# Retention as steps of one pipeline, with ACT and DVE in written order and each head's norm ahead of its output projection

## The chip, the cores and the metric

One core of a Trainium2 chip runs the whole kernel in one launch. The metric is the device time of that core in microseconds (us), the median over runs. Its engines work side by side, each through its own queue in order: TensorE (PE; its weight loads are shown as PEld), VectorE (DVE), ScalarE (ACT), GpSimd (POOL), and SyncE (SP), which here only issues DMAs. DMAs can be issued from the queues of SP, ACT and POOL. They meet at semaphores.

## The reference

A block of a transformer: a feed-forward part, a mixer, a second feed-forward part and a last norm, for 512 tokens behind 16 meta tokens (T = 528), width 1024, in fp32. The change lies in the mixer, in its retention:

```python
rq = rope(rq.reshape(B, T, RET_HEADS, RET_DK), pos)                       # 4 heads of 256
rk = rope(rk.reshape(B, T, RET_HEADS, RET_DK), pos) * (RET_DK ** -0.5)
yr = retention(rq, rk, rv)              # per head: (q k^T * decay) v, then per token
                                        # y = y * rsqrt(mean(y * y) + EPS) over the head's 512 columns
yr = (jax.nn.silu(rg) * yr) @ w_ret_out
...
ya = dsa_attention(aq, ak, av, iq, ik, iw, k_top) @ w_att_out
merged = jax.nn.sigmoid(g_ret) * yr + jax.nn.sigmoid(g_att) * ya
return merged @ w_mix_out
```

(axes' transpositions left out.) The attention picks for each query 128 keys by an index score of 8 small heads, `sum_h iw_h * relu(iq_h . ik)`; the score and the selection are computed beside the retention, ahead of the attention.

## The kernel before

All products are fp32 in three passes: each operand is split into a high part of the matmul's type and the rest (`split`: ACT copies the high part, DVE subtracts it, L117 and L118), and `mm3` (L145) adds high x high, high x low and low x high into PSUM. So each 128 columns of weights (`raw`, loaded by `load_w` on SP's queue, two buffers) go through one ACT and one DVE instruction to `whi` and `wlo` (three buffers each) ahead of their 24 matmuls.

The stages follow one another: feed-forward 1, the dense projections (values of retention and attention, index queries, queries and keys of head 0), the retention with index scores and selection beside it, the attention with its 8 heads, the output projections, feed-forward 2. In feed-forward and the dense projections the order of PE, ACT and DVE is written out (`manual_schedule(engines=BUSY)`): `steps_through` (L283) walks a list of steps, each with its load, its weights and its matmuls; while step i runs, step i+2's weights are split (the low part within the step, by `lower`) and step i+4's are loaded.

From the retention on, only PE's order is written; a scheduler places the instructions of ACT, DVE, POOL and the DMAs. Columns of weights come from `Cols.next`, which loads and splits. PSUM has 4 tiles of one bank (`sm_tile`) and 2 of two banks (`mm_tile`, for the 528-wide keys).

For each of the 4 heads the retention does: two query and two key projections (`psrq`, `psrk`); their ropes (`rope_pair`, L1415: four products each on DVE, two additions on POOL, splits to `rqk`); the scores with decay (`decayed`, L1454: five blocks `psst`, each multiplied by the table `u` on DVE and split); four gates (`psrg`, SiLU on ACT to `sg`); for each 128 of the head's 512 columns a weighing (`weigh`, L1486: 13 matmuls `pspv`, a square on ACT and its sum `ossum` on POOL, the product with the gate on DVE, and its split into `vo`). The head's norm `rn` needs the sums of all four (`rstd_steps` and `rstd_of`, L207 and L217: column sums `psn` on PE, mean on DVE, power on POOL, a diagonal split again, a broadcast `psn` by PE, a copy by ACT). As `rn` is one number per token, it can be applied behind the output projection: `ret_out` (L1426) does the 8 x 12 matmuls `psro` on the parts without the norm, DVE multiplies each result by `rn` (for head 0 into the accumulator `accr`, L1438, for the others into `tmp`, L1441), and POOL adds it (L1442). The last weighing and norm of a head run beside the next head's queries and keys.

Index work is placed by hand in PE's order, in pieces (`step`, `bg`): `index_ropes` (L1284) loads index queries and keys that the dense stage left in memory, with their tables, turns them by rope and splits them; `index_steps` (L1313) does 12 pairs of small score matmuls `pssc`, a ReLU of each on ACT (L1330) and a weighted sum on DVE (L1332); `select_steps` (L1337) does 48 rounds of maximum and replacement on DVE (L1344, L1345). The index tables and the decay are loaded from ACT's queue (L1275, L1530), the mask and the values from SP's.

Behind the retention, gates 2 and 3 of `g_ret` have been projected; the attention then projects a key, a query and a gate ahead of its first scores `psS`, and uses further gates as work to cover its softmax.

## Time and profile before

| what | value |
|---|---|
| time, median of 3 runs | 1565.4 us |
| the runs | 1565.08, 1565.40, 1567.57 us |
| the profiled execution, its time | 1567.74 us |
| its span, first to last instruction | 1566.0 us |
| granted TensorE clock, mean | 0.985 of full |
| busy, PE / DVE / ACT / POOL | 1528.2 / 1092.2 / 728.1 / 167.2 us |
| instructions | 24024 |

The page sums an execution; its parts are busy time per engine, the span in 40 slices, DMA queues, the chain of work that ended last (each piece led back to what released it), and the costliest groups of instructions. Further views list groups by line and shape, waits by who waited for whom, busy time by stretch with the granted clock, and the instructions in order of time. Matmuls overlap, so a busy PE need not be at its peak: the distance between the starts of one group's matmuls says more. An instruction's duration contains what its engine loses to others.

### The profile page before, as it was taken

Reading aid. Unit: us, or ns where it says so; the run is one execution under the profiler, and the core shown is the slowest. Engines: PE = TensorE matmul, PEld = TensorE weight load, DVE = VectorE, ACT = ScalarE, POOL = GpSimd, SP = SyncE. Lnnn points to the kernel's source line nnn. Section 1 sums busy time; section 2 is a strip of 40 time slices with the busy share of each in tenths; the row PEclk is TensorE's granted clock in tenths of the full one; section 3 lists DMA queues with packets and bytes.
Section 4 is the critical chain, followed back from the end, with each engine's and each line's share of the span. In section 5 each row is a group of like instructions: output and inputs, shape, how many; then the busy total and the mean of one; then the engine's idle time right before and its main releaser. Section 6 shows DMA issues by size and latency. Waiting matters only on the chain.

```text
span 1566.0 us, 24024 instructions
## 1 busy us (share of the span) xinstructions
PE 1528.2 (98%) x9779; PEld 1378.4 (88%) x9779; DVE 1092.2 (70%) x1656; ACT 728.1 (46%) x1145; POOL 167.2 (11%) x175
## 2 busy tenths in 40 slices
PE   9999999999999979999899999999999999999998
PEld 8999999999888866788787879989888889899996
DVE  4987585776877755796959376666455788576685
ACT  6555362554354444342333345666435445354453
POOL 1000000002110111103132171111001000000000
PEclk9999999999999998999999999999999999999999
DMA  4233233237364161241414142223443223323232
GB/s 164 73 117 103 87 102 115 82 126 241 120 229 154 72 200 52 82 131 44 145 44 135 54 138 81 68 84 84 152 132 130 81 81 109 108 82 135 81 109 94
DMA packets 154654, 172.97 MB, mean 110 GB/s; under 512 B 5040, under 2 KB 131016, under 8 KB 153776
## 3 DMA queue, kind: packets, MB, share of 16 engines
q1 hardware_dynamic: 144544, 148.81, 29.3%
q10 hardware_dynamic: 6592, 12.31, 2.4%
q0 software_dynamic: 3408, 10.32, 1.6%
q8 instruction: 76, 1.25, 0.3%
q14 instruction: 34, 0.28, 0.1%
HBM read 155.68 MB, written 15.75 MB: 109 GB/s over the span
## 4 chain that ended last, share of the span: by engine, by line
PE 86%; DVE 6%; POOL 2%; issue 2%; DMA 1%; ACT 1%; ACTq 0%; POOLq 0%; DVEq 0%
PE psqX L153 13%; PE psd L1859 7%; PE psd L153 7%; PE psqY L153 6%; PE psrg L153 5%; PE psvX L1111 4%; PE psqZ L153 3%; PE psrk L153 3%; PE psu L153 3%; PE psrq L153 3%; PE psga L153 3%; PE psmo L153 3%; PE psat L153 3%; PE psak L153 3%; PE psaq L153 3%; PE psgate L153 2%
## 5 line engine op out<-in xcount | busy, mean ns | idle before, releaser
L118 DVE TENSOR_TENSOR wlo<-raw,whi 128x1024 fp32r<-128x1024 f32 (+1 forms) x123 | 149.7, 1217 | 121.7 <-ACT whi L117 120.6
L117 ACT ACTIVATE whi<-raw 128x1024 fp32r<-128x1024 f32 (+1 forms) x123 | 115.3, 941 | 251.6 <-issue 41.2
L278 ACT ACTIVATE whi<-raw 128x1024 fp32r<-128x1024 f32 (+2 forms) x137 | 120.4, 880 | 110.1 <-PE psd L153 37.6
L279 DVE TENSOR_TENSOR wlo<-raw,whi 128x1024 fp32r<-128x1024 f32 (+2 forms) x137 | 139.9, 1026 | 29.9 <-ACT whi L278 29.9
L153 PE MATMUL psqX<-th,whi 128*128 128x264 f32 (+1 forms) x432 | 122.3, 283 | 0.1
L153 PE MATMUL psqX<-tl,whi 128*128 128x264 f32 (+1 forms) x432 | 122.3, 283 | 0.0
L153 PE MATMUL psqX<-th,wlo 128*128 128x264 f32 (+1 forms) x432 | 122.2, 283 | 0.0
L278 ACT ACTIVATE whi<-wsum 128x1024 fp32r<-128x1024 f32 x72 | 76.3, 1060 | 70.5 <-PE psd L1859 22.0
L279 DVE TENSOR_TENSOR wlo<-wsum,whi 128x1024 fp32r<-128x1024 f32 x72 | 87.9, 1222 | 12.5 <-ACT whi L278 12.5
L153 PE MATMUL psro<-vo,whi 128*128 128x512 f32 x256 | 81.2, 399 | 2.5 <-ACT tmp L1330 2.5
L153 PEld LDWEIGHTS psqX<-th,whi 128*128 128x128 f32 x432 | 82.1, 190 | 0.3 <-DVE g L492 0.3
L153 PEld LDWEIGHTS psqX<-th,wlo 128*128 128x128 f32 x432 | 82.0, 190 | 0.0
L153 PEld LDWEIGHTS psqX<-tl,whi 128*128 128x128 f32 x432 | 82.0, 190 | 0.0
L153 PE MATMUL psd<-hl,whi 128*128 128x264 f32 x352 | 71.2, 284 | 0.0
L153 PE MATMUL psd<-hh,wlo 128*128 128x264 f32 x352 | 70.9, 283 | 0.0
L153 PE MATMUL psd<-hh,whi 128*128 128x264 f32 x352 | 70.6, 282 | 0.0
L1859 PE MATMUL psd<-whi,hh 128*128 128x512 f32 x176 | 68.5, 389 | 0.0
L1859 PE MATMUL psd<-wlo,hh 128*128 128x512 f32 x176 | 68.5, 389 | 0.0
L1859 PE MATMUL psd<-whi,hl 128*128 128x512 f32 x176 | 68.5, 389 | 0.0
L252 POOL TENSOR_TENSOR ssum<-ssum,sq 128x528 f32<-128x528 f32 (+1 forms) x14 | 18.4, 1317 | 442.8 <-ACT sq L251 442.8
L153 PEld LDWEIGHTS psro<-vo,whi 128*128 128x128 f32 x256 | 49.2, 193 | 13.1 <-ACT tmp L1330 2.7
L153 PE MATMUL psrg<-xh,whi 128*128 128x512 f32 x128 | 53.5, 418 | 3.7 <-ACT tmp L1330 2.6
(432 smaller groups left out, 4620.2 us busy)
## 6 DMA issues: line engine op xcount, KB each, us to landing
raw<-in_ffn_w_up_dram SPq DMA_DIRECT2D x22, 1024.0 KB, 5.0
raw<-in_ffn_w_gate_dram SPq DMA_DIRECT2D x21, 1024.0 KB, 5.0
raw<-in_w_in_dram SPq DMA_DIRECT2D x19, 1024.0 KB, 5.1
raw<-in_w_in_dram SPq DMA_DIRECT2D x31, 512.0 KB, 3.4
raw<-in_ffn_w_down_dram SPq DMA_DIRECT2D x24, 512.0 KB, 3.4
w<-in_w_in_dram SPq DMA_DIRECT2D x24, 512.0 KB, 6.3
raw<-in_ffn_w_down_dram SPq DMA_DIRECT2D x12, 768.0 KB, 4.4
raw<-in_w_ret_out_dram SPq DMA_DIRECT2D x16, 512.0 KB, 3.4
```

Of the source, the lines that this page charges most:

```text
L117: nc.scalar.activation(hi, src, AF.Copy)
L118: eng.tensor_tensor(lo, src, hi.bitcast(F32), ALU.subtract)
L153: nc.tensor.matmul(o, a[:, k, :], b[:, sl], start=first and k == 0 and i == 0, stop=last and k == nk - 1 and i == 2, skip_group_check=onto)
L252: eng.tensor_tensor(ssum[:, :n], ssum[:, :n], sq[:, :n], ALU.add)
L278: nc.scalar.activation(hi, src, AF.Copy)
L279: return lambda: nc.vector.tensor_tensor(lo, src, hi.bitcast(F32), ALU.subtract)
L1111: nc.tensor.matmul(d[bank_][t], a, b[:, k, :], start=not onto and j + k + m == 0, stop=j + k == 3 and m == 2, skip_group_check=onto)
L1859: nc.tensor.matmul(ps, a[:, bs], m[:, j, :], start=first and i == 0, stop=last and i == 2)
```

## The change

The retention's projections, gates and outputs become steps of the pipeline that already runs feed-forward 1 and the dense stage, so the order of ACT and DVE is written out up to the end of the retention, and weights of one stage are split while the other's last steps run. Within it:

- A head's parts (`to`, four tiles) are kept unsplit behind the gate; when the norm `rn` is there, DVE multiplies each part by it and only then it is split into `vo` (`normed_parts`). The results of the output projection need no norm: ACT copies them for head 0, DVE adds them from PSUM onto the accumulator for the others. POOL does none of these additions.
- The sums of squares and the ropes' additions go from POOL to DVE.
- Output weights are split 256 columns at a time (4 x 256 in one instruction) in place of 128.
- The 12 index pairs stand within the matmuls of head 1's queries and keys (`between` in `mm3`, after k = 2, 4 and 7); ropes of index queries are done for all four at once, in four pieces beside head 0's gates. The selection's rounds stand at written places (`pick`).
- The order of a head: gates with their weighings; the next head's queries, the last weighing, column sums; keys, with the norm and the queries' rope; normed parts; output projection, with the keys' rope beside it; the next head's scores.
- Index tables, decay, mask, rope tables and values are loaded from SP's queue, index parts from POOL's (`bring_index`), in the first gate step.
- The retention's end also projects the first key, the first query and gate 4 of the attention stage, which before stood there.

```diff
@@ rstd_of
+        if late:
+            yield True
         nc.scalar.activation(dst, ps[:, :n], AF.Copy)
@@ mm3
         for k in range(nk):
+            for at, do in between:
+                if at == k:
+                    do()
@@ retention
-        def rope_pair(pa, pb, cs, sn, n, at):
...
-                nc.gpsimd.tensor_tensor(prod[u], prod[u], prod[v], op)
-                split(prod[u], *at[i])
...
-        def ret_out(h, o, rn, norm=iter(())):
...
-                    if h == 0:
-                        ins = nc.vector.tensor_tensor(acc_r[d], ps, rn, ALU.mult)
-                    else:
-                        t = tmp()
-                        ins = nc.vector.tensor_tensor(t[:, :S], ps, rn, ALU.mult)
-                        nc.gpsimd.tensor_tensor(acc_r[d], acc_r[d], t[:, :S], ALU.add)
...
+        def bring_index():
+            nc.sync.dma_start(ia[:, :, :NL], fq[:, :, :NL])
+            for r in range(4):
+                o = r ^ 1
+                nc.gpsimd.dma_start(ib[32 * r : 32 * r + 32, :, :NL], fq[32 * o : 32 * o + 32, :, :NL])
+            for i, t in enumerate((cosi, sini)):
+                nc.sync.dma_start(t, rope[0, i, :, REAL])
+            new_decay(0)
...
+        def index_queries(i):
+            late = slice(P, S)
+            a, b = ia[:, :, :NL], ib[:, :, :NL]
+            if i < 2:
+                t, tb = ((a, cosi), (b, sini))[i]
+                TT(t, t, tb[:, late].unsqueeze(1).to_broadcast([P, 4, NL]), ALU.mult)
+            elif i == 2:
+                TT(a, a, b, ALU.add)
+                nc.scalar.activation(iqh, a, AF.Copy)
+            else:
+                TT(iql, a, iqh.bitcast(F32), ALU.subtract)
...
+        def rope_pieces(pa, pb, cs, sn, n, at):
...
+            def first():
+                TT(new(0), pa, cs, ALU.mult)
+                TT(new(1), pb, sn, ALU.mult)
+                TT(d[0], d[0], d[1], ALU.subtract)
+                d["low"] = in_two(d[0], *at[0])
+
+            def second():
+                TT(new(2), pb, cs, ALU.mult)
+                TT(new(3), pa, sn, ALU.mult)
+                d["low"]()
+                TT(d[2], d[2], d[3], ALU.add)
+                d["low"] = in_two(d[2], *at[1])
+
+            return first, second, lambda: d["low"]()
...
+        def weigh(h, c):
+
+            d = heads[h]
+            ps = sm_tile("pspv")
+            weighted(ps, d["vs"][c], d["prob"])
...
+            t = rt.tile([P, S], F32, tag="to", name="to", bufs=4)
+            TT(t, ps, d["sg"][c], ALU.mult)
+            add_square(ps, d["ssum"], c == 0, rt, S, 1, nc.vector)
+            d["t"].append(t)
...
+        def normed_parts(h):
+
+            d, low = heads[h], lambda: None
+            for c in range(4):
+                TT(d["t"][c], d["t"][c], d["rn"], ALU.mult)
+                low()
+                o = tuple(p[:, c, :] for p in vr["parts"])
+                low = in_two(d["t"][c], *o)
+                d["o"].append(o)
+            low()
...
+        def gates_of(h):
+
+            def behind_0(ps):
+                silu(h, ps)
+                if h == 0:
+                    index_queries(0)
+                    index_queries(1)
+                else:
+                    pick(1)
+
+            def behind_1(ps):
+                if h == 0:
+                    index_queries(2)
+                    silu(0, ps)
+                    decayed(0)
+                    index_queries(3)
+                else:
+                    values_in(h)
+                    pick(1)
+                    silu(h, ps)
+                    weigh(h, 0)
...
+        def queries_keys(h):
...
+            def q0(ps):
+                pss["qa"] = ps
+                if not one:
+                    pick(2)
+                weigh(p, 3)
+
+            def q1(ps):
+                pss["qb"] = ps
+                if not one:
+                    pick(3)
+                norm_start(p)
+
+            def k0(ps):
+                pss["ka"] = ps
+                next(heads[p]["norm"])
+                ropes["q"] = rope_pieces(pss["qa"], pss["qb"], cos[:, REAL], sin[:, REAL], S, ret_q)
+                ropes["q"][0]()
+                ropes["q"][1]()
+                next(heads[p]["norm"])
+
+            def k1(ps):
+                pss["kb"] = ps
+                ropes["q"][2]()
+                normed_parts(p)
+                ropes["k"] = rope_pieces(pss["ka"], pss["kb"], cos, sin, T, ret_k)
...
+        def outputs(h, beside):
...
+                    for j in range(2):
+                        ps = sm_tile("psro")
+                        mm3([(ps, slice(0, S))], [t[:, :, j * P : (j + 1) * P] for t in w],
+                            lambda k: heads[h]["o"][k], DV // P)
...
+                        if j == 0:
+                            lower()
+                            beside(i)
+                    for j, ps in enumerate(pss):
+                        a = acc_r[2 * i + j]
+                        if h == 0:
+                            nc.scalar.activation(a, ps, AF.Copy)
+                        else:
+                            TT(a, ps, a, ALU.add)
+                    if i == 3 and h + 1 < RH:
+                        decayed(h + 1)
...
+        more = gates_of(0)
+        for h in range(1, RH):
+            more += queries_keys(h) + outputs(h - 1, beside_outputs(h - 1)) + gates_of(h)
...
+        steps += more
+        with tc.manual_schedule(engines=BUSY):
+            for _ in range(4):
+                next(pipe)
...
+        with tc.manual_schedule(engines=BUSY):
+            for _ in pipe:
+                pass
+            for _ in picks["steps"]:
+                pass
```

More of the change, by code (lines that the diff above doesn't have):

```diff
@@ L311, in steps_through @@
             yield
-        for i in range(len(steps)):
+        i = 0
+        while i < len(steps):
             pre(i + 4)
@@ L533 @@
     fp = f1s.enter_context(pool("f1"))
-    with ExitStack() as later:
+    later = ExitStack()
+    if True:
         plain_ps = ExitStack()
@@ L1311 @@
-    wt = bp.tile([P, 4, IH], F32, tag="wt", name="wt")
     def index_steps():
@@ new lines, in pair, with proj, run, steps_of @@
+        def pair():
+            next(picks["pairs"], None)
+        def proj(name, sl, between, behind):
+            def run(w, lower):
+                if sl is None:
+                    outs, ps = halves(mm_tile(name))
+                else:
+                    ps = sm_tile(name)
+                    outs = [(ps, sl)]
+                mm3(outs, w, xs, KD, between=between)
+                lower()
+                behind(ps)
+            return run
+        def steps_of(tiles_, runs):
+            return [(*t, r, 0) for t, r in zip(tiles_, runs)]
@@ new lines @@
+        dense.close()
+        later.close()
+        tp["make"] = None
+        sel = ExitStack()
+        bp = sel.enter_context(pool("bp", 1, side="right"))
+        bias = [bp.tile([P, NM + P * (j + 1)], F32, tag=f"bias{j}", name=f"bias{j}") for j in range(4)]
+        score = [None] + [bp.tile([P, P * (j + 1)], F32, tag=f"score{j}", name=f"score{j}") for j in range(1, 4)]
+        caus = bp.tile([P, S], F32, tag="caus", name="caus")
+        gap(bp, 8)
+        ixs = ExitStack()
+        ix = ixs.enter_context(pool("ix", 1, side="right"))
```

428 lines of the change are left out of this document (212 added, 216 removed).

## The prediction

> **What bounds the kernel now.** I read the page first, then the chain of waits, then busy time by stretch, then what PE waited for.
>
> ```profile
> span 1566.0 us, 24024 instructions
> ...
> PE 1528.2 (98%) x9779; PEld 1378.4 (88%) x9779; DVE 1092.2 (70%) x1656; ACT 728.1 (46%) x1145; POOL 167.2 (11%) x175
> ...
> PE 86%; DVE 6%; POOL 2%; issue 2%; DMA 1%; ACT 1%; ACTq 0%; POOLq 0%; DVEq 0%
> ```
>
> PE is the bound, but not of all of the span: 14% of the chain lies elsewhere. The change touches only the retention, from the first `psrg` (555.40) to the first attention scores (938.29). What that stretch would take at full pace follows from groups that ran without a gap:
>
> ```profile
> 502.90 5.44 PE psvX L1111 x24
> ...
> 629.15 1.02 PE psn L214 x8
> ...
> 672.22 4.05 PE psst L1463 x30
> ...
> 806.15 11.66 PE psrk L153 x96
> ...
> 860.84 1.96 PE pspv L1483 x12
> 862.81 5.57 PE psrg L153 x24
> ```
>
> ```profile
> 611.40 0.72 PE pssc L1327 x6
> ```
>
> A 512-wide matmul takes 5.44/24 = 0.227 us, a 264-wide one 11.66/96 = 0.121 us. The code gives the counts: 1008 of the first kind (gates, queries, outputs, the first attention query) make 228.5; 336 of the second (keys) 40.8; 16 weighings 31.4; 4 score blocks 16.2; 4 norms (1.02 + two of 0.227) 5.9; 12 index pairs at no more than 0.72, 8.6; the rest some 2. Sum 333.4 us.
>
> ```profile
> 555.40:596.18 40.78, 29.06 (x132) 22.64 (x130) 22.77 (x32) 17.21 (x27) 4.26 (x14) 0.86 0.64 202
> 596.18:647.47 51.29, 46.91 (x277) 38.85 (x278) 32.00 (x46) 20.34 (x39) 12.24 (x11) 0.93 0.10 31
> 647.47:762.46 114.99, 109.70 (x555) 93.46 (x555) 94.87 (x160) 38.14 (x57) 22.44 (x19) 0.96 0.32 107
> 762.46:848.31 85.85, 82.03 (x428) 70.88 (x429) 64.56 (x112) 28.24 (x44) 22.30 (x19) 0.98 0.28 92
> 848.31:938.29 89.98, 86.94 (x414) 73.69 (x415) 52.38 (x82) 37.01 (x55) 32.87 (x28) 0.96 0.32 102
> sum 382.89, PE 354.64 PEld 299.52 DVE 266.59 ACT 140.94 POOL 94.11; mean PE 70.93 PEld 59.90 DVE 53.32 ACT 28.19 POOL 18.82
> ```
>
> Columns: length, then busy time (instructions) of PE, PEld, DVE, ACT, POOL, then the granted clock. It took 382.9, so 49.5 us are waits and slow clock: this is all that the change can win. Two reasons stand out:
>
> ```profile
> PE pssc L1327 <- ACT ikh L1308: 8.3, 1, 8.3
> PE psst L1463 <- DVE tmp L1441: 5.7, 2, 3.2
> PE psS L1661 <- ACT aq L117: 3.0, 1, 3.0
> ...
> PE psrg L153 <- ACT tmp L1330: 2.6, 1, 2.6
> PE psro L153 <- ACT tmp L1330: 2.5, 1, 2.5
> ```
>
> ```profile
> 596.18 8.48 PE psrg L153 x24
> ```
>
> Whole waits of 2.5 us and more, and after each the clock is low: 24 matmuls took 8.48 instead of 5.57 us. Second, output projections go at the pace of DVE, which POOL slows:
>
> ```profile
> 722.86 0.68 DVE L118 TENSOR_TENSOR wlo<-raw,whi 128x512 fp32r<-128x512 f32 x1
> 723.46 0.68 DVE L118 TENSOR_TENSOR rqk<-tmp,rqk 128x512 fp32r<-128x512 f32 x1
> ...
> 748.44 1.53 DVE L118 TENSOR_TENSOR wlo<-raw,whi 128x512 fp32r<-128x512 f32 x1
> ```
>
> The same split takes 0.68 alone (the next one starts 0.60 later) and 1.53 beside POOL's additions.
>
> **The change part by part.** PE's matmuls stay, in another order; so the sum is one of waits.
>
> ```profile
> L118 DVE TENSOR_TENSOR wlo<-raw,whi 128x1024 fp32r<-128x1024 f32 x36 | 48.8, 1355 | 45.8 <-ACT whi L117 44.8 <-PE psPT L1677 1.0
> ...
> L1441 DVE TENSOR_TENSOR tmp<-psro,rn 128x512 f32<-128x512 f32 x24 | 16.1, 678 | 0.0
> ...
> L1344 DVE MAX8 top<-score 128x8 f32<-128x512 f32 x16 | 11.0, 688 | 0.2
> ...
> L1345 DVE MATCH_REPLACE8 score<-top,score 128x512 f32<-128x512 f32 x16 | 10.8, 678 | 0.0
> ...
> L1332 DVE SCALAR_TENSOR_TENSOR score<-tmp,wt,score 128x256 f32<-128x256 f32 x7 | 4.4, 629 | 0.4
> ...
> L1294 DVE TENSOR_TENSOR iqa<-iqa,cos 128x768 f32<-128x768 f32 x2 | 1.9, 959 | 5.3 <-DMA cos<-in_rope_dram 2.8 <-DMA iqa<-fq 2.5
> ```
>
> ```profile
> L1442 POOL TENSOR_TENSOR accr<-accr,tmp 128x512 f32<-128x512 f32 x24 | 36.2, 1516 | 37.4 <-DVE tmp L1441 37.4
> ...
> L223 POOL TENSOR_TENSOR rcol<-ms,mhalf 128x4 f32<-128x4 f32 x4 | 4.4, 1112 | 13.8 <-DVE ms L221 13.8
> ```
>
> *Load of DVE.* It gains 16 norm multiplications of the heads' parts, 12 rope additions and 12 sums of squares (40 at 0.68 = 27); it loses the 8 multiplications of head 0 (5.4). The 24 additions onto the accumulator replace 24 multiplications one for one. With POOL out, 36 splits go from 1.355 to some 1.2, twice the 0.60 above (about 5), and 32 narrow output splits (0.68 to 1.53) become 16 wide ones (about 15). Net near zero: some 268 of 333 us. On the sum DVE isn't the bound; what counts is where its written order makes PE wait. Where PE runs ahead of no one, these edits cost nothing: in an output step DVE has 1.2 + 3 x 0.68 + 2 x 0.68 = 4.6 under PE's 5.44, in a gate step 1.2 + 2 x (0.69 + 0.68) + 2 x 0.68 = 5.3 under 5.44 + 1.96. ACT's 8 extra copies for head 0 (under 0.63 each) lie under the same steps. I walk the four places where it does not fit.
>
> *(a) The start.* Index tables, decay and values, before on ACT's queue, now stand on SP's, behind one wait:
>
> ```profile
> 557.12 8.41 DMA vst<-part
> ```
>
> ```profile
> 565.60 0.33 ACTq L1275 DMA_DIRECT2D sin<-in_rope_dram  x1
> ```
>
> ```profile
> u<-in_decay_dram ACTq DMA_DIRECT2D x4, 384.0 KB, 3.1
> ...
> sin<-in_rope_dram ACTq DMA_DIRECT2D x1, 256.0 KB, 2.7
> ```
>
> The tables lie where the values' last store is read from, which ends at 565.5; then they are issued and take 2.7 us: 568.3. DVE, in written order, does two index products (1536 wide, twice 0.96 each: 3.8), a split 1.2, a sum 1.9, and only then the first score block's product 0.6: 575.9. PE has done two gates and three score blocks by 569.6 and has no free PSUM tile (four, two of them gates): it waits 6.3. The third gate waits for the second SiLU behind a 1536-wide ACT split: 0.9. The clock falls: about 2. The values' low halves stand behind an index split: 0.9. Sum 10. Queued behind SP's waiting table are decay, values, mask and one weight load; that one is needed two steps later. Bounds: 5 (PE waits for one product) to 17 (the first stretch today: 40.8 less 23.7 of matmuls).
>
> *(b) Keys of head 1, with the index pairs between.* DVE owes, ahead of the norm's broadcast, six score steps (0.63 each, 3.8, and 1.7 behind from the steps before), a split 1.2, diagonal and its split 1.4 with ACT's part 0.63: 8.7 with hand-offs 11.5; PE has keys and pairs, 5.8 + 1.5 = 7.3. Wait 4. Then seven rope products 4.4, six score steps 3.8, splits 1.8, eight norm steps 4.8 and 2 of ACT between, 16.8; PE has 5.8 + 1.2 + 2.7 = 9.7. Wait 7. With slow clock 2: 13. Bounds 4 (the broadcast alone) to 24.
>
> *(c) Keys of heads 2 and 3.* The same without pairs:
>
> ```profile
> L117 ACT ACTIVATE vo<-tmp 128x512 fp32r<-128x512 f32 x16 | 10.1, 632 | 11.9 <-DVE tmp L1491 11.9
> ```
>
> From the end of the norm's column sums: the mean 0.2 (after five selection rounds of 0.69 + 0.68, so some 0.6 late), a split 1.2 that hides POOL's power (1.1), diagonal 0.7, ACT 0.63, low half 0.7, seven rope products 4.3, ACT's split 0.63 and norm copy 0.6, then eight norm steps 4.8 and 0.6 for the first part: 15. PE has 5.8 + 0.5 + 5.8 + 2.7 = 14.8, but can't do the output's first block until the parts are there, one after another: wait 1.5 a head, 3 in all; spread, so no slow clock. Bounds 0 to 7 each (today's two waits for scores, 5.7, with some slow clock).
>
> *(d) The end.* Last norm without ropes: DVE is done before PE's query projection. Two gates (10.9) then cover the first attention rope: tables 2.7 to 3.1, POOL's gates and product, split; some 12. Wait 2 (today 3.0 and slow clock). Bounds 0 to 6.5 (3.0, and one low stretch).
>
> *Hand-offs* between engines that I didn't count: 3, of the chain's "issue" (2% of 1566 is 31 over the whole span, this stretch is a quarter of it, and half of it stays).
>
> Sum: 10 + 13 + 3 + 2 + 3 = 31 in place of 49.5, a gain of 18.5. The profiled execution took 1567.7 (span 1566.0 and 1.7 around it), so 1549.2; it lies 2.3 above the median of the three runs, 1565.4. Against that: **1547**.
>
> What low clock costs goes by the rows above: every whole wait of 2.5 us and more has one. The Trainium skill ("TensorE: Matmul & The Clock Gate", What's actually happening) lets the clock fall after one idle free-running window of some 3.4 us; by that, waits under that length would sometimes go free, and the sum would be some 2 us lower. The trace does not agree to the letter: waits of 2.5 and 2.6 us were followed by low clock, which a mean over a window would explain better than one idle window.
>
> **The rivals.**
> *PE-bound throughout*: DVE starts each instruction 0.60 after the last, and hides (b) to (d) but for 2 us. For it: DVE has 65 us to spare over the stretch. Against it: the order at (b) holds seventeen steps in one line. Only (a), 2 and hand-offs stay, 15: 49.5 - 15 = 34.5 of gain, 1531.
> *The waits move, no more*: (a) stays as long as today's first stretch, 17, and (b) as long as today's second, which has 51.3 for some 40 of matmuls, 11.5, plus 5 of slow clock: 17 + 16.5 + 3 + 2 + 3 = 41.5; gain 8, 1557. For it: the cause of the 8.3 wait, tables behind a store of values, stands in the new order too.
> *Slower: selection rounds ahead of the norm.* Each norm stands behind five selection rounds in written order, where a scheduler could let it pass. If DVE comes L late to the mean, PE waits L more in one piece ahead of the outputs, and pays the low clock as well, 8.48 - 5.57 = 2.9, in three heads. It decides from 3 x (L + 2.9) = 18.5, L = 3.3 us (two and a half rounds). At L = 6: 26.7, 8 us slower, 1573. For it: rounds wait for nothing and fill DVE early. Against it: my steps have 5.3 of DVE under 7.4 of PE, so it should catch up.
> That the change doesn't do what it says is no rival: the written order is what the queues get, and PE's instructions are the same in number.
>
> **How the numbers follow.** Forecast 1547 (1540 to 1553) 0.50; PE-bound 1531, 0.14; moved waits 1557, 0.19; slower 1573, 0.13; as before 0.04. A measurement of this kernel can tell about 0.2%, 3 us. Faster: the first three less some of the third's upper end, 0.80; same 0.07; slower 0.13. All bounds at their ends give gains of 40 and -12 (1525 to 1577); 8 in 10 lie between **1532 and 1565**.
>
> **What would show it.** POOL has next to no additions in the stretch, and splits of 0.68 us next to none of 1.5 (right), output projections at 2.72 per 12 matmuls. (a): PE's longest wait is a score block for DVE some 14 us after the first gate. (b): `psn` broadcast waits for DVE's low half near 4, the first `psro` of head 0 for low halves near 6. (c): under 2 for later heads. Wrong it is if PE waits over 5 us in heads 2 or 3, if the granted clock of the stretch is under 0.93, or if time outside the stretch moves by over 3 us.

## The result, and the profile after

The changed kernel takes 1562.7 us (median; 1560.8 to 1563.2) against 1565.4 beside it: 0.998 of the time before, 95% interval 0.9972 to 0.9989. The forecast was 1547, a gain of 18.5; the gain is 2.7 by the medians and 4.7 by the profiled spans. The head and the engines' row of the page, after:

```profile
span 1561.3 us, 23921 instructions
...
PE 1527.3 (98%) x9779; PEld 1374.8 (88%) x9779; DVE 1092.4 (70%) x1670; ACT 728.7 (47%) x1138; POOL 105.7 (7%) x135
```

PE and DVE do as much as before; POOL lost 61.5 us, its additions. So the loads are as the prediction had them, and the question is the waits. What PE waited for from 550 to 945 (in total, how many times, the longest), after:

```profile
PE psro L157 <- ACT vo L284: 9.5, 3, 3.7
PE psst L1435 <- DVE tmp L1439: 9.0, 1, 9.0
PE psn L242 <- ACT tmp L117: 3.1, 1, 3.1
PE psS L1834 <- ACT aq L117: 1.0, 1, 1.0
PE psro L157 <- DVE vo L285: 0.7, 3, 0.2
```

The 8.3 for the first index pair is now 9.0 for a score block; the 5.7 at the later heads' score blocks is gone, and 9.5 at the first output blocks stands in its place. The stretch by the prediction's parts, after (length, busy time of PE, PEld, DVE, ACT and POOL, granted clock, then DMA's share and GB/s):

```profile
555.56:599.66 44.10, 35.09 (x167) 29.81 (x166) 24.08 (x31) 17.17 (x26) 8.11 (x22) 0.88 0.63 191
599.66:646.64 46.98, 40.18 (x245) 31.03 (x243) 29.69 (x47) 18.53 (x37) 2.57 (x4) 0.96 0.17 60
646.64:733.63 86.99, 83.72 (x429) 71.56 (x429) 58.92 (x95) 31.37 (x47) 3.51 (x4) 0.96 0.27 91
733.63:819.00 85.37, 82.55 (x429) 70.44 (x429) 62.36 (x104) 27.14 (x39) 3.45 (x4) 0.98 0.27 92
819.00:901.68 82.68, 82.35 (x405) 69.23 (x406) 59.06 (x107) 28.82 (x40) 1.85 (x1) 0.98 0.28 92
901.68:936.34 34.66, 33.44 (x146) 26.68 (x144) 29.18 (x54) 13.75 (x18) 13.14 (x16) 1.00 0.37 103
```

At the prediction's prices for a matmul the first row's work is 31.7 us (four gates, the score blocks, three weighings), the second's 34.7, the third's and fourth's 79.5 each (outputs, score blocks, four gates, four weighings, queries, norm, keys), the fifth's 79.1, the last's 32.7. Over it go 12.4, 12.3, 7.5, 5.9, 3.6 and 2.0.

The stretch up to the second `psaq` (938.29 before, where the prediction ends it) lasted 382.9 before and 383.8 after (555.4 to 939.2), but it now holds one attention gate more (24 matmuls, 5.45), which before came later. So its waits and slow clock fell from 49.5 to 383.8 - 338.9 = 44.9, not to 31.

Heads 1 and 2 show what took the place of what. Before, the output blocks ran on into the score blocks, and those waited (`psst` to the next gate, 4.05 at full pace):

```profile
752.44:762.46 10.02, 4.75 (x32) 3.95 (x30) 10.02 (x16) 2.60 (x4) 2.60 (x3) 0.83 0.51 171
839.89:848.31 8.42, 4.60 (x31) 3.93 (x30) 8.42 (x16) 2.75 (x4) 2.56 (x2) 0.97 0.58 193
```

After, the first of these takes 4.1, but the keys (first window of each pair: from the first `psrk` to the first `psro`) and the outputs (second) are longer:

```profile
757.97:762.07 4.10, 4.10 (x32) 3.82 (x31) 2.89 (x6) 1.17 (x2) 0.00 (x0) 1.00 0.26 91
```

```profile
717.97:733.63 15.66, 12.38 (x100) 11.97 (x99) 11.70 (x20) 4.25 (x8) 1.94 (x1) 1.00 0.17 57
733.63:757.97 24.34, 24.11 (x97) 18.89 (x98) 19.52 (x28) 7.03 (x9) 0.00 (x0) 0.93 0.32 105
804.17:819.00 14.83, 12.25 (x100) 11.96 (x99) 10.91 (x19) 4.23 (x8) 1.87 (x1) 1.00 0.17 59
819.00:843.32 24.32, 24.10 (x97) 18.91 (x98) 19.25 (x28) 7.04 (x9) 0.00 (x0) 0.93 0.32 107
```

Keys and broadcast are 12.1 of matmuls: 3.6 and 2.7 lie over it, nearly all of it waits for `vo` (3.3 and 2.6). The 96 output matmuls need 21.8 at full clock; here they took 24.3, and the granted clock of 0.93 accounts for 1.7 of the 2.5 over it (0.07 x 24.3). That is 11.3 for two heads (3.6 + 2.5 + 2.7 + 2.5), where the prediction had 3; the two score blocks gave back 10.3 (10.02 + 8.42 before, 4.10 + 4.08 after).

Why the parts were late is seen on DVE, ACT and PE at the end of head 3's keys, beside which head 2's norm runs (start, length; in brackets the idle time ahead and what ended it):

```profile
805.02 0.15 DVE L225 TENSOR_SCALAR ms<-psn 128x4 f32<-128x4 f32 x1
805.09 1.21 DVE L285 TENSOR_TENSOR wlo<-raw,whi 128x1024 fp32r<-128x1024 f32 x1
807.22 0.69 DVE L232 TENSOR_TENSOR tmp<-ident,rcol 128x512 f32<-128x512 f32 x1 [0.92 <-POOL rcol L227]
...
815.76 1.23 DVE L285 TENSOR_TENSOR wlo<-raw,whi 128x1024 fp32r<-128x1024 f32 x1 [2.13 <-ACT whi L284]
816.91 0.69 DVE L285 TENSOR_TENSOR rqk<-tmp,rqk 128x512 fp32r<-128x512 f32 x1
817.51 1.29 DVE L1487 TENSOR_TENSOR to<-to,rn 128x512 f32<-128x512 f32 x2
```

```profile
814.21 0.58 ACT L245 ACTIVATE rn<-psn 128x512 f32<-128x512 f32 x1
814.68 1.05 ACT L284 ACTIVATE whi<-raw 128x1024 fp32r<-128x1024 f32 x1
818.23 1.24 ACT L284 ACTIVATE vo<-to 128x512 fp32r<-128x512 f32 x2 [2.50 <-DVE to L1487]
```

```profile
818.91 0.50 PE L157 MATMUL psro<-vo,whi 128*128 128x512 f32 x1 [2.58 <-ACT vo L284]
```

The norm `rn` is there at 814.8. But in written order a split of later weights, those of the second output step, comes first: ACT copies its high half, DVE sits idle until that is done (2.13) and subtracts (1.23), and only then multiplies the first part. ACT, idle for 2.50, copies that part to `vo`, and PE has waited 2.58. From mean to first part it is one chain through DVE, POOL, ACT and PE, in which DVE isn't busy but late.

### The profile page after: what moved, and what is told of

Its sections match the earlier page's. It is cut to its first block, busy times and chain, and to the rows that moved or that the text cites. A ratio compares the mean times of both kernels' runs of the same rounds, so it can differ in the third digit from the quotient of the medians.

```text
span 1561.3 us, 23921 instructions
## 1 busy us (share of the span) xinstructions
PE 1527.3 (98%) x9779; PEld 1374.8 (88%) x9779; DVE 1092.4 (70%) x1670; ACT 728.7 (47%) x1138; POOL 105.7 (7%) x135
## 4 chain that ended last, share of the span: by engine, by line
PE 85%; issue 7%; DVE 4%; ACT 2%; DMA 1%; POOL 1%; POOLq 0%; ACTq 0%; DVEq 0%
PE psqX L157 13%; PE psd L157 8%; PE psd L2035 7%; PE psqY L157 7%; PE psro L157 4%; PE psvX L1120 4%; PE psrg L157 4%; PE psqZ L157 3%; PE psu L157 3%; PE psga L157 3%; PE psmo L157 3%; PE psat L157 3%; PE psak L157 3%; PE psaq L157 2%; PE psg L157 2%
## 5 line engine op out<-in xcount | busy, mean ns | idle before, releaser
L285 DVE TENSOR_TENSOR wlo<-raw,whi 128x1024 fp32r<-128x1024 f32 (+2 forms) x184 | 197.4, 1076 | 65.7 <-ACT whi L284 65.6
L284 ACT ACTIVATE whi<-raw 128x1024 fp32r<-128x1024 f32 (+2 forms) x184 | 170.0, 925 | 135.3 <-PE psd L157 41.2
L118 DVE TENSOR_TENSOR wlo<-raw,whi 128x1024 fp32r<-128x1024 f32 (+1 forms) x60 | 72.3, 1205 | 56.7 <-ACT whi L117 55.7
L117 ACT ACTIVATE whi<-raw 128x1024 fp32r<-128x1024 f32 (+1 forms) x60 | 62.6, 1045 | 93.9 <-PE psat L157 26.6
L285 DVE TENSOR_TENSOR wlo<-wsum,whi 128x1024 fp32r<-128x1024 f32 x72 | 87.9, 1222 | 12.5 <-ACT whi L284 12.5
L157 PE MATMUL psro<-vo,whi 128*128 128x512 f32 x256 | 86.0, 415 | 10.2 <-ACT vo L284 9.5
L157 PEld LDWEIGHTS psd<-hh,wlo 128*128 128x128 f32 x352 | 54.4, 188 | 0.0
L157 PEld LDWEIGHTS psd<-hh,whi 128*128 128x128 f32 x352 | 54.3, 188 | 0.0
```

Of the source, the lines that this page charges most:

```text
L117: nc.scalar.activation(hi, src, AF.Copy)
L118: eng.tensor_tensor(lo, src, hi.bitcast(F32), ALU.subtract)
L157: nc.tensor.matmul(o, a[:, k, :], b[:, sl], start=first and k == 0 and i == 0, stop=last and k == nk - 1 and i == 2, skip_group_check=onto)
L284: nc.scalar.activation(hi, src, AF.Copy)
L285: return lambda: nc.vector.tensor_tensor(lo, src, hi.bitcast(F32), ALU.subtract)
```

## The experiments

Each was timed beside the kernel before, which took 1564.7 to 1565.0 us there. Ratios are to it; the changed kernel stands at 0.998. The intervals are 1.3 to 2.4 us to either side, so a difference of a microsecond or two between runs says little. Theory A: the waits are the length of chains in written order. B: DVE has no time to spare. C: selection rounds ahead of the norm set it, the prediction's slower rival.

**The next weights' low half behind the normed parts.**

```diff
 def proj(name, sl, between, behind, late=False):
...
         mm3(outs, w, xs, KD, between=between)
-        lower()
+        if not late:
+            lower()
         behind(ps)
+        if late:
+            lower()
...
-  proj("psrk", None, THREE if one else (), k1)])
+  proj("psrk", None, THREE if one else (), k1, True)])
...
-  [proj("psaq", REAL, (), last_3)]
+  [proj("psaq", REAL, (), last_3, True)]
```

> Edit: in the second key step of heads 1 to 3 (and the step before the last head's outputs) the low half of the next output step's weights is written by DVE after the normed parts, not before them. Theory A (the wait at the first output block is the length of a chain of steps in written order, not a lack of DVE time): in the changed kernel DVE sat idle 2.13 us for that split's high half, then took 1.1 for the low half, and only then multiplied by the norm. Without it the three waits of psro for ACT's vo (9.5 us in all, about 3.2 each) fall to about 1 each, and low clock behind them goes too: 6 to 9 us faster than the changed kernel's 1562.7, so 1554 to 1557. Rival B (DVE has no time to spare there): the low half is then late for the second output block, and PE waits there for wlo as long: 1561 to 1564. Rival C (selection rounds ahead of the norm set it): the normed parts still wait for the norm's broadcast, under 2 us gained.

Measured: 1555.2 us, ratio 0.9941 (0.9929 to 0.9953): 7.5 faster than the changed kernel, as A had it. DVE in the same head:

```profile
800.54 0.15 DVE L225 TENSOR_SCALAR ms<-psn 128x4 f32<-128x4 f32 x1
...
809.85 0.69 DVE L285 TENSOR_TENSOR rqk<-tmp,rqk 128x512 fp32r<-128x512 f32 x1 [0.70 <-ACT rqk L284]
810.46 1.29 DVE L1487 TENSOR_TENSOR to<-to,rn 128x512 f32<-128x512 f32 x2
```

From mean to first part it is 9.9 us instead of 12.5. PE's three waits for `vo`, 9.5, became two, the longer of them at head 0:

```profile
PE psro L157 <- ACT vo L284: 3.2, 2, 2.5
```

The place of one split in each head's order, with the same work done, is worth 7.5 us.

**Selection rounds behind the norm's mean.**

```diff
 def q1(ps):
     pss["qb"] = ps
-    if not one:
-        pick(3)
     norm_start(p)
+    if not one:
+        pick(3)
...
 def last_1(ps):
+    norm_start(RH - 1)
     pick(3)
     keep_gate(ps)
-    norm_start(RH - 1)
```

> Edit: in the second query step of heads 2 and 3 and in the second gate step ahead of the last head's norm, the three selection rounds stand behind the norm's mean instead of ahead of it; nothing else moves. Theory A (the rounds cost only the 1.1 us by which the mean was late in the trace of head 2): 1 to 2 us faster a head where PE waits, 2 to 4 in all, 1558.5 to 1561. Rival C (rounds ahead of the norm are the cause, L of 3 us and more a head): 6 to 10 us faster, 1553 to 1557. Rival D (the rounds now delay the diagonal by as much as they delayed the mean): no change, 1562 to 1564.

Measured: 1567.4, ratio 1.0018 (1.0009 to 1.0026): 4.7 slower than the changed kernel. None of the theories had that sign. The trace says why (mean and diagonal of head 2):

```profile
804.81 0.16 DVE L225 TENSOR_SCALAR ms<-psn 128x4 f32<-128x4 f32 x1 [2.78 <-PE psn L218]
...
809.65 0.68 DVE L232 TENSOR_TENSOR tmp<-ident,rcol 128x512 f32<-128x512 f32 x1
```

The three rounds (3.6 us) now stand between mean and diagonal: 4.8 us apart instead of 2.2. DVE now sits idle for 2.78 ahead of the mean, where the rounds had been, and does them in the chain. D, that they would delay the diagonal, had the mechanism, with too small a price. C gets nothing from it.

**Ten selection rounds left out.** To separate C and B from A, this kernel leaves out the five rounds in the two query steps of each of heads 2 and 3:

```diff
 def q0(ps):
     pss["qa"] = ps
-    if not one:
-        pick(2)
     weigh(p, 3)
...
 def q1(ps):
     pss["qb"] = ps
-    if not one:
-        pick(3)
     norm_start(p)
...
-    for _ in range(TOPK // 8):
+    for _ in range(TOPK // 8 - (3, 3, 4)[j - 1]):
```

> Edit: this kernel leaves out 10 of the 48 selection rounds: the five that stand in the two query steps ahead of the norm in each of heads 2 and 3. Theory A (rounds are late by 1.1 us at the mean, and the rest of the wait is the chain behind it): 1 to 2 us faster a head, 1558.5 to 1561. Rival C (rounds ahead of the norm are what PE waits for; moved behind the mean they only delayed the diagonal instead): the psro waits of heads 1 and 2 fall from 3.5 and 2.8 to under 1, 6 to 10 us faster, 1553 to 1557. Rival B: DVE has 14 us less to do, which shows as some 10 us in all the waits together.

Measured: 1562.4, ratio 0.9988 (0.9979 to 0.9996), the changed kernel's time within the error. The waits for `vo` fell from 9.5 to 7.6, not under 1; heads 1 and 2 still had one of 2.0 each, and the clock behind it stayed low (waits, then the outputs of heads 1 and 2):

```profile
PE psro L157 <- ACT vo L284: 7.6, 3, 3.7
```

```profile
732.09:756.95 24.86, 24.42 (x98) 19.20 (x98) 19.42 (x29) 6.97 (x9) 0.00 (x0) 0.93 0.33 103
817.35:841.89 24.54, 24.08 (x98) 19.10 (x98) 19.16 (x29) 6.98 (x9) 0.00 (x0) 0.93 0.33 106
```

C falls: without any round ahead of it the norm is still late. B loses its ground too: from 599.66 to 936.34 DVE was busy for 228.7 us instead of 239.2, and the time didn't move. A's 1 to 2 us a head did not show either: shorter waits, the same low clock (the last section says from what gap on PE pays it).

**The next head's first gate ahead of the outputs.** It leaves the chain as it is and gives PE 24 matmuls to do meanwhile:

```diff
-    more += queries_keys(h) + outputs(h - 1, beside_outputs(h - 1)) + gates_of(h)
+    gates = gates_of(h)
+    more += queries_keys(h) + gates[:1] + outputs(h - 1, beside_outputs(h - 1)) + gates[1:]
...
-    return steps_of(tiles(("rg", h), w_in, OFF_RG + h * DV, 4), runs)
+    if h == 0:
+        return steps_of(tiles(("rg", h), w_in, OFF_RG, 4), runs)
+    at = OFF_RG + h * DV
+    return steps_of(tiles(("rg0", h), w_in, at, 1) + tiles(("rg", h), w_in, at + P, 3), runs)
```

> Edit: the first gate step of each head 1 to 3 (psrg, 24 matmuls, 5.4 us of PE) stands between the keys and the outputs of the head before, in place of behind those outputs. Theory A (latency of the norm's chain): PE has 5.4 us of other work while the chain ends; the waits at the first psro (9.5) and within its 24 matmuls (some 2.5 a head), with low clock behind them, go for all three heads; 10 to 15 us faster, 1548 to 1553. Rival B (DVE has no time to spare in the stretch): the wait comes back at the next head's scores or weighings; under 4 us gained, 1559 to 1563. Slower is possible if the fifth gate's SiLU or the weights' buffers now block: over 1565.

Measured: 1546.5, ratio 0.9889 (0.9874 to 0.9904): 16.2 faster than the changed kernel, past A's range. Keys with the gate, and outputs, of heads 1 and 2:

```profile
712.14:729.78 17.64, 17.64 (x123) 16.48 (x123) 13.69 (x23) 5.21 (x9) 1.94 (x1) 1.00 0.27 97
729.78:751.77 21.99, 21.99 (x97) 18.04 (x96) 19.45 (x30) 7.27 (x9) 0.00 (x0) 1.00 0.33 98
792.54:810.07 17.53, 17.53 (x123) 16.49 (x123) 13.61 (x23) 5.61 (x10) 1.87 (x1) 1.00 0.29 97
810.07:832.06 21.99, 21.99 (x97) 18.05 (x96) 18.41 (x29) 6.87 (x9) 0.00 (x0) 1.00 0.35 99
```

PE is busy for the whole of each window and the clock is 1.00; the 24.3 of the outputs is 22.0. DVE does the same work and doesn't hold PE up anywhere else. B falls here for the later heads.

**The norm put behind the projection again.** One part of the change undone:

```diff
 def weigh(h, c):
...
-    add_square(ps, d["ssum"], c == 0, rt, S, 1, nc.vector)
-    d["t"].append(t)
+    o = tuple(p[:, c, :] for p in vr["parts"])
+    low = in_two(t, *o)
+    add_square(ps, d["ssum"], c == 0, rt, S, 1, nc.vector)
+    low()
+    d["o"].append(o)
...
-    normed_parts(p)
...
-    normed_parts(RH - 1)
...
+    rn = heads[h]["rn"]
     if h == 0:
-        nc.scalar.activation(a, ps, AF.Copy)
+        TT(a, ps, rn, ALU.mult)
     else:
-        TT(a, ps, a, ALU.add)
+        t = rt.tile([P, S], F32, tag="to", name="to", bufs=4)
+        TT(t, ps, rn, ALU.mult)
+        TT(a, a, t, ALU.add)
```

> Edit: one part of the change undone: the heads' outputs are split without their norm as soon as they are weighed, and the norm is multiplied onto the output projection again (DVE multiplies and adds, POOL stays out). Theory A (the norm's chain, when it stands ahead of the projection, is what PE waits for): the psro waits for vo (9.5 us, and some 2.5 a head within the first block, with low clock) go for all heads; in their place DVE has 1.2 + 3 x 0.68 + 4 x 0.68 = 6.0 under an output step's 5.44, about 0.5 x 12 = 6 more: 10 to 14 gained less 6, so 1555 to 1559. Rival B (DVE's time over the stretch is the limit): 16 more multiplications of 0.68 show in full, 1568 to 1575. Rival F (the projection waits for free PSUM because the norm is late anyway): the same time as the changed kernel, 1561 to 1564.

Measured: 1553.0, ratio 0.9931 (0.9919 to 0.9943): 9.7 faster than the changed kernel, though DVE has 16 multiplications more, and 2 beyond A's range. PE waits for no `vo` any more; a wait at the first attention scores grew from 1.0 to 3.8. So the rest of the change (steps, written order, additions on DVE) is worth some 12 us against the 1564.7 of the kernel before beside it, and the norm ahead of the projection, in the place it has, costs 10 of them.

**POOL's power twice**, in the changed kernel and in the one with the gate first:

```diff
+    if late:
+        twice = sp.tile([P, 5], F32, tag="rtwice", name="rtwice", bufs=1)
+        nc.gpsimd.tensor_tensor(twice[:, :nb], ms[:, :nb], mhalf[:, :nb], ALU.pow)
     nc.gpsimd.tensor_tensor(r[:, :nb], ms[:, :nb], mhalf[:, :nb], ALU.pow)
```

> Edit: the changed kernel, and POOL's power twice, as in the run before. Theory A (the chain from the mean to the parts is on the path in heads 0, 1 and 2): 1.0 to 1.9 a head appears in full, with more low clock: 3 to 7 us slower than 1562.7, so 1566 to 1570; the psro or psn waits are longer by as much. Rival B (DVE's time is the limit): POOL's power lies beside DVE's work, no change, 1561 to 1564.5.

> Edit: the gate run, and POOL raises each head's mean to its power twice (the first result is not used), so the norm's chain is 1.0 to 1.9 us longer in each of four heads. Theory A (the gate covers the chain): within 2 us of 1546.5. Rival B (DVE, not the chain, sets the pace): also within 2; the two are told apart only together with the next run.

Measured without the gate: 1567.8, ratio 1.0015 (1.0007 to 1.0024), 5.2 slower than the changed kernel, in A's range. The trace shows it less plainly than A had it: the span grew by 3.8 (1565.1 against 1561.3), PE's recorded waits by 1.4 in all, and the outputs of head 2 ran at a clock of 0.88 instead of 0.93 (26.3 us instead of 24.3). With the gate: 1548.8, ratio 0.9894 (0.9881 to 0.9908), 2.4 slower than without the second power by the medians, just past A's 2, and 0.05% by the ratios, whose intervals overlap. PE's waits for the norm's broadcast, which stands ahead of the gate, grew there from 3.1 to 4.7. The instruction, four of each, in the first of the two:

```profile
L229 POOL TENSOR_TENSOR rtwice<-ms,mhalf 128x4 f32<-128x4 f32 x4 | 6.6, 1661 | 107.0 <-DVE ms L225 107.0
...
L230 POOL TENSOR_TENSOR rcol<-ms,mhalf 128x4 f32<-128x4 f32 x4 | 4.0, 1001 | 0.0
```

Four times 1.0 us on an engine that is 7% busy cost 5 us where nothing covers the chain, and at most 2.4 where the gate covers most of it. B said no change in both.

**The start.** The index queries behind the first weighings, with buffers of their own:

```diff
 def bring_index():
+    new_decay(0)
...
-    new_decay(0)
...
 behind_0, h == 0:
-    index_queries(0)
-    index_queries(1)
 behind_1, h == 0:
-    index_queries(2)
     silu(0, ps)
     decayed(0)
-    index_queries(3)
 behind_2, h == 0:
     silu(0, ps)
-    for i in range(3):
-        index_keys(i)
+    index_queries(0)
+    index_queries(1)
 behind_3, h == 0:
     weigh(h, 2)
+    index_queries(2)
+    index_queries(3)
+    for i in range(3):
+        index_keys(i)
```

> Edit: at the start the first head's scores are decayed and weighed ahead of the index queries' rotation, which moves to the third and fourth gate step (with buffers of its own), and the decay table is the first load issued. Theory A (PE's 9.0 us at the score block is DVE held in written order behind the index tables' landing at 571.9): the wait for tmp at psst falls from 9.0 to under 3, the low clock behind it (10 us at half speed) is gone or short; 6 to 9 us faster, 1553.5 to 1557. Rival B (DVE lacks time over the first four gates, so what is moved makes PE wait later, at the weighing or at the index pairs): the wait turns up there, change within 2 us, 1561 to 1565. Rival E (the values, which come from the same store, are what is late): the wait moves to the first pspv, gain of 2 to 5, 1558 to 1561.

Measured: 1562.7, ratio 0.9992 (0.9983 to 1.0001), nothing gained. The 9.0 at the score block is gone, and in its place:

```profile
PE pssc L1252 <- ACT ikh L1379: 8.0, 1, 8.0
```

B had the outcome, but its reason is not what the trace shows: DVE sat idle for 4.0 us twice ahead of the index steps and again between them (1.55 and 0.69 for ACT's halves); what is late is again a chain in written order, seven index steps and two more weighings to `ikh`.

Then also the twelve pairs one step later:

```diff
-THREE = ((2, pair), (4, pair), (7, pair))
+THREE = ((1, pair), (3, pair), (5, pair), (7, pair))
...
-  [proj("psrq", REAL, THREE if one else (), q0), proj("psrq", REAL, THREE if one else (), q1)]
+  [proj("psrq", REAL, (), q0), proj("psrq", REAL, THREE if one else (), q1)]
```

> Edit: as in the run with the index queries late, and the twelve index pairs of PE begin one step later (none in head 1's first query step, four in each of the next three). In that run the 9.0 us wait of psst had turned into 8.0 of the first pair for ACT's ikh. Theory A' (DVE's chain of index steps from the tables' landing on is about 5 us longer than PE's work up to the first pair, and the wait goes if the first pair is asked for 6 us later): PE waits under 3 at pssc, 5 to 8 us faster than 1562.7: 1555 to 1558. Rival B (DVE is short of time up to the first outputs): the wait moves on to the norm of head 0, psn or psro there over 5 us longer, gain under 2.

Measured: 1563.6, ratio 0.9992 (0.9983 to 1.0). A' falls, and B's place, the norm of head 0, is not where the wait went either (`psn` 3.5 instead of 3.1, the first output blocks unchanged at 9.5). The last weighing's PSUM tile is now read by DVE only behind those index steps, and the first pair waits for that tile instead:

```profile
PE pssc L1252 <- ACT sq L257: 5.4, 1, 5.4
```

With the gate first, the index late and the pairs spread over the second query step, the keys and the gate (the two diffs above, `THREE` as in the changed kernel, also on the gate step of head 1):

> Edit: the first gate step of the next head ahead of each head's outputs, the index queries behind the first weighings, and the twelve index pairs spread over head 1's second query step, both key steps and that gate step, three in each. Theory A (each of the stretch's waits is a latency that PE can cover with a step that is ready): the gate run's 1546.5 less the 8.8 at psst and the low clock behind it: 1535 to 1540, and no wait of PE over 3 us in the stretch. Rival B (DVE is short of time by then): a wait comes back at head 1's keys, and it is 1542 to 1547.

Measured: 1550.9, ratio 0.9916 (0.9903 to 0.9929), 4.4 slower than the gate alone. Two waits at pairs (4.7 and 4.2) took the place of the 8.8, and the psn wait grew to 3.5. Neither theory's range has it; the sign is B's.

**Pairs out of the first key step.** With the gate first:

```diff
-  [proj("psrk", None, THREE if one else (), k0), ...
+  [proj("psrk", None, (), k0), ...
...
-    runs = [proj("psrg", REAL, (), b) for b in (behind_0, behind_1, behind_2, behind_3)]
+    runs = [proj("psrg", REAL, THREE if h == 1 and b is behind_0 else (), b)
+            for b in (behind_0, behind_1, behind_2, behind_3)]
```

> Edit: the gate run (1546.5), and three of the twelve index pairs moved from head 1's first key step to the gate step that follows the keys. It prices the wait of psn for the broadcast's high half (3.1 us and 3.4 of slow clock), which the prediction put on DVE's score steps ahead of the norm. Theory A: it goes, 1541 to 1544. Rival G (the wait is the chain of mean, power, diagonal and halves itself, not the score steps): it stays over 2 us, 1545 to 1548.

Measured: 1548.0, ratio 0.9890 (0.9876 to 0.9903), no gain: G's range, not A's. The wait of `psn` (3.1) did go, so G is wrong about its cause; but a pair in the gate step now waits longer, for a ReLU that ACT does behind its copies of the normed parts:

```profile
PE pssc L1252 <- ACT tmp L1255: 4.2, 1, 4.2
```

**The index steps between.** Gate first, those pairs moved, and the index sums and splits right behind the first weighing (taken out of the places where they stood; the decay's load and the buffers as in the run with the index late):

```diff
 behind_1, h == 0:
     silu(0, ps)
     decayed(0)
+    index_queries(0)
+    index_queries(1)
 behind_2, h == 0:
     weigh(0, 0)
     silu(0, ps)
-    for i in range(3):
-        index_keys(i)
+    index_queries(2)
+    index_keys(0)
+    index_keys(1)
+    index_queries(3)
+    index_keys(2)
```

> Edit: the gate step of the next head first, as before (1546.5); at the start the decay table is the first load, the first head's scores are decayed before the index products, the index sums and splits stand right behind the first weighing (not behind the last, as in the run with the index late), and the twelve index pairs leave head 1's first key step for that gate step. Theory A' (at the start DVE's chain of index steps can lie under the third and fourth gate): the 8.8 at psst goes, at most 3 come back at the first weighing or the first pair, and psn's 3.1 goes with the pairs: 1535 to 1541. Rival B (as in the two index runs, the chain only moves its wait): a wait of over 5 us at a weighing or a pair, 1544 to 1549.

Measured: 1539.2, ratio 0.9835 (0.9822 to 0.9849), in the range of A'; it beats the kernel before by 25.8 us and the changed one by 23.5. PE's waits of the stretch:

```profile
PE pssc L1252 <- ACT tmp L1255: 4.3, 1, 4.3
PE pspv L1457 <- DVE vo L285: 1.3, 1, 1.3
PE psS L1842 <- ACT aq L117: 0.9, 1, 0.9
```

Against the run before it (0.9890) only the order and buffers of the start differ: 0.55% or 8.6 us, the price of the 9.0 wait when the index steps have a place where PE has work over them. One wait at a pair is left, untried.

## Why the prediction was wrong

The direction was right, and the stretch is where the change acts: outside it, 1561.3 - 939.2 + 5.45 = 627.6 against 1566.0 - 938.3 = 627.7. The sum was not: 44.9 us of waits and slow clock, not 31. The time lies within the range of 1532 to 1565, near its slow end.

| term | forecast | found | from |
|---|---|---|---|
| (a) start | 10 | 12.4 | first window over its matmuls |
| (b) keys of head 1 and what follows | 13 | 15.7 | second window 12.3; head 0's outputs 25.15 - 21.8 = 3.4 |
| (c) heads 2 and 3 | 3 | 11.3 | the two pairs of windows |
| (d) end | 2 | 2.0 | last window |
| hand-offs | 3 | 3.5 | the rest of 44.9 |

Head 0's outputs, after:

```profile
646.64:671.79 25.15, 25.15 (x97) 20.01 (x98) 14.96 (x21) 10.65 (x16) 0.00 (x0) 0.88 0.29 92
```

**Load of DVE**, right: 263.3 us in the six windows (268 forecast for the stretch), and splits no longer slowed by POOL. The output steps could keep PE's pace too: with the gate first they did, at 22.0. Order, not load, decided.

**(a)**, nearly right in size and place. The wait at the score block is 9.0, not 6.3, because the index tables took longer to land than in the row of before, 2.7 (the same loads after: KB each, median us from issue to landing):

```profile
cos<-in_rope_dram SPq DMA_DIRECT2D x1, 256.0 KB, 6.2
sin<-in_rope_dram SPq DMA_DIRECT2D x1, 256.0 KB, 6.4
```

Issued at 565.6 among the other loads of the start, they held DVE until 571.9 (568.3 forecast). The two runs that moved that work showed what the sum could not: this wait is worth its length only if DVE's order lets the index steps end elsewhere in time.

**(b)**, right in place; that the size nearly fits is partly luck. `psn` waited 3.1 (4 forecast) and the first output block 3.7 (7 forecast), so 4.2 less in waits. The slow clock, put at 2, took more: 3.4 over full pace in head 0's outputs alone, 3.0 of it by the granted 0.88. And PE was busy for 40.2 in the second window, where full pace gives 34.7: the clock there (0.96) accounts for under 2 of that, and the rest goes with the index pairs between matmuls, which took from 0.72 to 1.28 each, where the prediction put them at no more than 0.72.

**(c)** is the step that failed, 8 of the 14 us: "wait 1.5 a head, 3 in all; spread, so no slow clock". By the prediction's own terms the first part is ready for PE 10.8 us after the column sums (its 15 less the eight norm steps, plus one of them), within the 12.1 that PE has; in the trace of head 2 it took 14.7 (from 804.17, where the keys begin, to 818.91). Three things were off. The split of the second output step's weights was left out of the chain, 1.05 on ACT and 1.23 on DVE, between norm and first part; moving its second half alone, in every head, gave 7.5 us. POOL's power, "a split 1.2 that hides POOL's power (1.1)", took 1.9 beside that split, so it was not hidden; doubling it, in every head, cost 5.2. And the wait came in one piece, 3.3 and 2.6, not spread, so the clock fell in the outputs of both heads (0.93). In size, the norm ahead of the projection costs 9.7 by the run that undid it.

**(d)** and the rest came out as forecast.

The rivals: PE-bound throughout is out as the change was written, but the run with the gate first came within a microsecond of the forecast by covering (c); that it meets the number is chance, as it is another order. Of those with a mechanism "the waits move, no more" (1557) was nearest, right in kind and wrong in place: it put them at (a) and (b), and it was the waits at the score blocks of heads 2 and 3 that moved, to the outputs of heads 1 and 2 just ahead of them. The slower rival, rounds ahead of the norm, is refuted: leaving ten of them out gave nothing. Of the signs named, a score block as the longest wait came out, POOL's additions were gone, (c) "under 2" failed, and so did "output projections at 2.72 per 12 matmuls" (24.3 for 96 is 3.04). The three conditions for being wrong did not come true (no wait over 5 us in heads 2 and 3, clock 0.96, outside 0.1 us): they were too wide for an error made of two waits of 3 us and the slow clock behind them.

The Trainium skill ("TensorE: Matmul & The Clock Gate", What's actually happening) lets the clock fall after one idle window of some 3.4 us; to the letter, a wait shorter than that would always go free, not only sometimes. By the traces here 2.0 us of recorded wait sufficed (the windows at 0.93 in the run with ten rounds left out), so a wait of 2 to 3 us cost about twice its length, the low clock and late parts behind it included, as the forecast's own row had it.

## What to carry to other kernels

When a step is put ahead of a matmul that waited for less before, follow the chain from its first instruction to the matmul through every queue, with all that stands in written order between, also what belongs to other steps (here the next weights' split); sums of busy time by engine don't show it. If the chain is longer than what PE still has to do, look for a step that is ready and put it between: that gave 16 us where shortening the chain gave 7.5. A wait that is only made shorter can keep its low clock, so follow it down to where that goes too. A wait that vanishes at one place is a gain only once the places behind it in the same order are seen not to wait.

## What the runs showed of the hardware

POOL's power on four columns takes 1.0 us by itself and 1.9 when a split of DVE with two SBUF inputs has begun just before it. Head 0 (no DVE instruction beside it) and head 2 (DVE's split at 805.09 to 806.30) of the changed kernel:

```profile
622.20 1.04 POOL L227 TENSOR_TENSOR rcol<-ms,mhalf 128x4 f32<-128x4 f32 x1 [9.48 <-DVE ms L225]
```

```profile
805.32 1.87 POOL L227 TENSOR_TENSOR rcol<-ms,mhalf 128x4 f32<-128x4 f32 x1 [5.60 <-DVE ms L225]
```

DVE's split, 1.21, wasn't slowed. 1.87 is what is left of that split, 0.98, and 0.9 of its own, as if POOL stood still until DVE was done. The Trainium skill ("SBUF — State Buffer", SBUF: two separate sides) has it so: DVE instructions with two SBUF inputs and POOL share a pair of ports, whoever starts first holds it for the whole instruction, and the other is blocked. The trace agrees, and so does the split of 1.53 us beside POOL's additions in the kernel before. A small POOL instruction in a chain is therefore not hidden by such a split of DVE that began just before it, but queued behind it.

A gap of 2.2 us in PE's work brought half clock, one of 1.7 us did not. In the fourteen traces of this case (the first 20 us and all behind 1500 us left out), wherever two matmuls started 2.2 us or more apart, the granted clock fell to 0.50 during the gap or within about 2 us of its end, for 3.4 us or two or three times that; gaps from 0.9 to 1.7 us brought none (two of 1.0 lay in a stretch that a longer gap had brought). Between 1.7 and 2.2 no trace has a gap. One such stretch, in head 1's outputs of the changed kernel:

```profile
734.75:738.16 3.41, 3.41 (x9) 2.12 (x8) 3.06 (x6) 2.21 (x3) 0.00 (x0) 0.50 0.35 120
```

These 3.4 us at half clock cost 1.7. That fits the two runs that shortened the waits of heads 1 and 2: with ten rounds left out the gaps fell from 3.6 and 2.9 to 2.2 and the low stretches stayed, with the low half moved they fell to 1.0 and less and the stretches were gone. The traces show no reason for the bound.
